# Running logsumexp over rows: first rows looked at by ScalarE, and another order of tile sizes

## The chip, the cores and the metric

The kernel runs on one NeuronCore of a Trainium2 chip. The metric is the device time of one execution in microseconds (us), lower is better. Beside the timed runs there is a profiled execution, whose trace holds each engine's instructions and the packets of the DMA engines. The engines are TensorE (PE in the profile), VectorE (DVE), ScalarE (ACT), GpSimd (POOL) and SyncE (SP), which here issues all transfers.

## What is computed

The input x has 4 batches of 4096 rows with 4128 columns, float32. Each output row is the logsumexp of all input rows up to it, column by column:

```python
out[:, 0, :] = x[:, 0, :].copy()
for t in range(1, S):
    mx = np.maximum(out[:, t - 1, :], x[:, t, :])
    out[:, t, :] = mx + np.log(np.exp(out[:, t - 1, :] - mx) + np.exp(x[:, t, :] - mx))
```

That is log(cumsum(exp(x))) over the rows. The input is 270.5 MB and so is the output; each is moved once.

## The kernel before, in words

**Tiles.** A batch's 4096 rows are cut into tiles of 2 or 3 blocks; a block is 128 rows. A tile of r blocks takes 128*r rows, and each of the 128 partitions holds r neighbouring rows of it (`dram`, L76). The class `Step` is such a tile: `b` is its batch, `row` its first row, `r` its number of blocks, and `first` and `last` say whether it begins or ends a batch. The lists `usual` (batches 0 to 2) and `final` (batch 3) give the sizes, in blocks, in order (L144 to L150). There are 49 tiles: 19 of two blocks and 30 of three. In this text tile 0 is the first, and load t and store t are its transfers.

**Buffers.** Four tiles are in the chip's SBUF at a time (`SLOTS`). Every fourth tile comes from the pool `x2`, which has room for two blocks, the others from `x3` with three buffers of three blocks.

**Work on one tile.** The columns are cut into three chunks of 1376 (`Chunk`). For each:
- `exp` (L97): ScalarE replaces the tile by its exponentials. In the first tile of a batch, the first row is also looked at: GpSimd compares its exponentials with 2^-63 (L99, into `ample`) and multiplies the answers into `least` (L103), so that `least` tells at the end whether any was too small.
- `sums` (L109, L111): VectorE adds the rows that lie in one partition, into `z` of this chunk. For three blocks L109 adds the first two in place, then L111 adds the last.
- `head` (L119): TensorE multiplies `z` by a triangular matrix, which gives each partition the sum of all rows before its own. In the first tile of a batch the matrix is `below`, in later ones `carried`, which also takes up the running sum that the tile before left in the last partition of `z`. The result is in PSUM (`pt`, two buffers). For a chunk these are two float32 products of 512 columns and one of 352, which the profile counts as six matmuls.
- `add` (L128, L136; in the last tile of a batch L131 in place of L136): VectorE adds that base to the tile's rows and puts the last row of each partition into `z`. L131 also adds up the result into `probe`.
- `log` (L141, L142): ScalarE takes the logarithm of all rows but the partition's last from the tile, and of the last from `z`, in place.

**What sets the order.** The order is written out by hand (`manual_schedule`), one list for each engine. ScalarE's list goes: for tile t, exp of chunk 2, log of chunk 0, exp of chunk 0 of the next tile, log of chunk 1, exp of chunk 1 of the next tile, log of chunk 2. VectorE's and TensorE's lists go beside it (L177 to L182). Every engine works its list in order. A look on GpSimd is issued with its `exp`, and VectorE's additions that overwrite the looked-at row come after it.

All transfers are issued by SP, in the order of `moves`: the loads of the first four tiles; store 0; store 1; and from there a load, three tiles ahead, behind each store. A store waits for the tile's three logarithms; a load waits for the store of the tile that had its buffer. An issue that waits holds back all that stand behind it in SP's list.

**At the end** (L213 to L234) the minimum over `least` (L215) and a comparison of `probe` with 2^62 (L218) go into the table `fits`, whose minimum over all partitions decides a flag. If the flag is set, a slow general version (`_general`) computes everything again; with the input at hand it is not.

Of the kernel before, what the change touches and what calls it, by code (L numbers as in the profile page):

```python
# [7 lines left out]
FP32 = mybir.dt.float32  # L8
I32 = mybir.dt.int32
ACT = mybir.ActivationFunctionType  # L10
ALU = mybir.AluOpType
AX = mybir.AxisListType
P = 128
MM = 512
NC = 3
SLOTS = 4
SMALL = 2.0 ** -63
LARGE = 2.0 ** 62
# [3 lines left out]
def kernel(  # L22
# [5 lines left out]
    nc = tc.nc  # L28
    B, S, D = x.shape
    assert S % P == 0 and D % (NC * 32) == 0  # L30
    CH = D // NC
# [3 lines left out]
    consts = ctx.enter_context(tc.tile_pool(name="consts", bufs=1))  # L35
# [10 lines left out]
        out=below, in_=below, pattern=[[1, P]], compare_op=ALU.is_ge,  # L46
# [5 lines left out]
        out=carried, in_=below, pattern=[[0, P]], compare_op=ALU.not_equal,  # L52
# [4 lines left out]

    probe = consts.tile([P, B * NC], FP32, name="probe")
    nc.gpsimd.memset(probe, 1.0)
    least = consts.tile([1, CH], FP32, name="least")  # L60
    nc.gpsimd.memset(least, 1.0)  # L61
    ample = consts.tile([1, CH], FP32, name="ample")

    z = [zpool.tile([P, CH], FP32, name=f"z{c}") for c in range(NC)]
    for t in z:
# [23 lines left out]
    class Chunk:  # L89
# [4 lines left out]
        def exp(self):  # L94
            t = self.t
            e = t.xt[:, :, self.cols]
            nc.scalar.activation(e, e, ACT.Exp)  # L97
            if t.first:
                nc.gpsimd.tensor_scalar(  # L99
                    out=ample, in0=t.xt[0:1, 0, self.cols], scalar1=SMALL, scalar2=None,  # L100
                    op0=ALU.is_ge,
                )
                nc.gpsimd.tensor_tensor(out=least, in0=least, in1=ample, op=ALU.mult)  # L103

        def sums(self):
            r = self.t.r
# [34 lines left out]
            nc.scalar.activation(e, e, ACT.Ln)  # L141
            nc.scalar.activation(t.xt[:, r - 1, self.cols], self.z, ACT.Ln)  # L142

    usual = [2, 3, 3, 3, 2, 3, 2, 3, 2, 3, 3, 3]  # L144
    final = [2, 3, 2, 3, 2, 2, 3, 2, 2, 3, 3, 3, 2]
    steps = []
    for b in range(B):
        parts = final if b == B - 1 else usual
        row = 0
        for i, r in enumerate(parts):  # L150
            if row == S:
                break
            pool = x3 if len(steps) % SLOTS else x2
            steps.append(Step(b, row, r, pool, row + P * r == S))
            row += P * r
        assert row == S
# [41 lines left out]
    while any(at[e] < len(l) for e, l in lists.items()):  # L198
        before = len(done), sum(at.values())
        for e, l in lists.items():  # L200
            while at[e] < len(l):
                op = l[at[e]]
# [7 lines left out]
        assert before != (len(done), sum(at.values()))  # L210


    fits = consts.tile([P, B * NC + 1], FP32, name="fits")  # L213
    nc.vector.memset(fits[:, B * NC:], 1.0)
    nc.vector.tensor_reduce(  # L215
        out=fits[0:1, B * NC:], in_=least, op=ALU.min, axis=AX.X,
    )
    nc.vector.tensor_scalar(  # L218
        out=fits[:, :B * NC], in0=probe, scalar1=LARGE, scalar2=None, op0=ALU.is_le,
    )  # L220
    low = consts.tile([P, 1], FP32, name="low")
    nc.vector.tensor_reduce(out=low, in_=fits, op=ALU.min, axis=AX.X)  # L222
# [4 lines left out]
        out=flag, in0=good, scalar1=float(P), scalar2=None, op0=ALU.is_lt,  # L227
# [68 lines left out]
```

## Time and profile before

| | |
|---|---|
| time, median of 3 runs | 1275.89 us (1275.76 to 1276.1) |
| profiled execution | 1275.27 us |
| span of its instructions | 1273.6 us |
| VectorE busy | 993.9 us, 548 instructions |
| ScalarE busy | 938.3 us, 442 instructions |
| TensorE matmuls busy | 609.9 us |
| GpSimd busy | 108.7 us, of it L99 57.9 us (12 times) and L103 45.0 us (12 times) |
| moved by DMA | 541.29 MB, 425 GB/s over the span |
| granted TensorE clock, mean | 0.69 |

The span goes from the first to the last instruction of the profiled execution; the rest of that execution's time, 1.67 us, lies around it. Busy time is the sum over an engine's instructions, and engines work at the same time, so the busy times do not add up to the span. In the profile a line such as `xt<-pt,xt` names the tile written and the tiles read. The time of a transfer is counted on 16 DMA engines; a DMA share of 1.00 in a stretch means that all 16 had packets throughout. (In stretches of one or two us a share can pass 1, because a packet counts where it starts.)

The most frequent instructions, by shape: Exp of three blocks takes 3633 ns and of two blocks 2486 ns (L97); the logarithm 2494 ns on two rows per partition and 1343 ns on one (L141), and 1335 ns from `z` (L142); VectorE's additions of 1376 columns take 1583 ns (L128 with one row per partition) and with two rows 3018 ns.

### The profile page before, as it was taken

How to read it: one execution, taken by the hardware profiler on the slowest of the kernel's cores; microseconds unless marked ns; L12 is line 12 of the kernel's file. 1: busy time of each engine (PE TensorE's matmuls, PEld its weight loads, DVE VectorE, ACT ScalarE, POOL GpSimd, SP SyncE). 2: the span in 40 equal slices, each digit the busy share in tenths (PEclk: the TensorE clock that was granted, in tenths of full speed). 3: DMA queues.
4: the chain of work that ended last, by engine and by line, in shares of the span. 5: the costliest groups of instructions: out<-in, count | busy, mean ns of one | idle time of the engine just before them, and what ended most of it. 6: DMA issues, size and time to landing. Idle time of an engine off the chain costs nothing.

```text
span 1273.6 us, 3466 instructions
## 1 busy us (share of the span) xinstructions
PE 609.9 (48%) x884; PEld 237.6 (19%) x884; DVE 993.9 (78%) x548; ACT 938.3 (74%) x442; POOL 108.7 (9%) x37
## 2 busy tenths in 40 slices
PE   2555445445445444644544545443553455362552
PEld 1222112212112111211211212111221122121220
DVE  4998668779779676867977959666997696784894
ACT  3798778678668677768956868766886686795894
POOL 6200000001600000000340000000043000000000
PEclk9667667666666767766666766776666767686676
DMA  9979999999999999999999999999999999999998
GB/s 407 420 318 422 425 437 429 434 431 426 439 433 427 431 433 429 438 430 437 431 430 433 431 433 432 433 433 429 434 440 425 439 429 435 425 411 415 429 442 345
DMA packets 14132, 541.29 MB, mean 425 GB/s; under 512 B 1568, under 2 KB 1568, under 8 KB 1568
## 3 DMA queue, kind: packets, MB, share of 16 engines
q1 hardware_dynamic: 14112, 541.07, 98.9%
q8 instruction: 7, 0.11, 0.0%
q14 instruction: 13, 0.11, 0.0%
HBM read 270.53 MB, written 270.53 MB: 425 GB/s over the span
## 4 chain that ended last, share of the span: by engine, by line
DMA 66%; DVE 19%; ACT 12%; issue 1%; PE 1%; SPq 0%; ACTq 0%; DVEq 0%
DMA xt<-in_x_dram 54%; DMA out_dram<-xt 13%; DVE xt L128 7%; ACT xt L97 5%; DVE z L111 5%; ACT xt L141 4%; DVE z L136 3%; DVE xt L109 3%; ACT xt L142 2%; PE pt L119 1%; DVE z L131 0%; SPq L87 0%; ACTq L141 0%; ACTq L97 0%; SPq L84 0%
## 5 line engine op out<-in xcount | busy, mean ns | idle before, releaser
L119 PE MATMUL pt<-z,carried 128*128 128x512 f32 (+1 forms) x810 | 557.3, 849 | 581.4 <-DVE z L111 581.4
L97 ACT ACTIVATE xt<-xt 128x4128 f32<-128x4128 f32 (+1 forms) x147 | 468.5, 3189 | 237.7 <-DMA xt<-in_x_dram 237.7
L119 PEld LDWEIGHTS pt<-z,carried 128*128 128x128 f32 x810 | 216.8, 285 | 922.0 <-issue 917.6
L128 DVE TENSOR_TENSOR xt<-pt,xt 128x2752 f32<-128x2752 f32 (+1 forms) x147 | 361.8, 2461 | 0.7 <-PE pt L119 0.7
L141 ACT ACTIVATE xt<-xt 128x2752 f32<-128x2752 f32 (+1 forms) x147 | 301.0, 2048 | 81.3 <-DVE z L136 76.3
L111 DVE TENSOR_TENSOR z<-xt 127x1376 f32<-127x1376 f32 x147 | 259.8, 1768 | 58.2 <-ACT xt L97 54.6
L109 DVE TENSOR_TENSOR xt<-xt 128x1376 f32<-128x1376 f32 x90 | 145.7, 1619 | 199.5 <-ACT xt L97 199.5
L136 DVE TENSOR_TENSOR z<-xt 128x1376 f32<-128x1376 f32 x135 | 224.2, 1660 | 4.6
L142 ACT ACTIVATE xt<-z 128x1376 f32<-128x1376 f32 x147 | 196.3, 1335 | 0.0
L99 POOL TENSOR_SCALAR ample<-xt 1x1376 f32<-1x1376 f32 x12 | 57.9, 4827 | 855.8 <-ACT xt L97 855.1
L119 PE MATMUL pt<-z,below 128*128 128x512 f32 (+1 forms) x72 | 52.4, 895 | 60.6 <-DVE z L111 60.6
L103 POOL TENSOR_TENSOR least<-least,ample 1x1376 f32<-1x1376 f32 x12 | 45.0, 3750 | 1.0
L119 PEld LDWEIGHTS pt<-z,below 128*128 128x128 f32 x72 | 20.7, 306 | 91.8 <-issue 70.8
L131 DVE CUSTOM_DVE_ANT_0 z<-xt 128x1376 f32<-128x1376 f32 x12 | 19.1, 1592 | 0.4
L66 POOL MEMSET z<- 128x1376 f32 x3 | 3.7, 1235 | 0.0
L224 PE MATMUL good<-ones,low 128*1 128x1 f32 x2 | 0.2, 164 | 5.6 <-DVE low L222 5.6
L34 ACT ACT_TABLE_LOAD x1 | 1.3, 1283 | 0.8 <-PEq L280 0.8
L215 DVE TENSOR_REDUCE fits<-least 1x1 f32<-1x1376 f32 x1 | 1.6, 1575 | 0.1
L224 PEld LDWEIGHTS good<-ones,low 128*1 128x1 f32 x2 | 0.1, 80 | 6.2 <-DVE low L222 6.2
L61 POOL MEMSET least<- 1x1376 f32 x1 | 1.2, 1235 | 0.0
L131 DVE DVE_READ_ACCUMULATOR2_ANT probe<- 128x1 f32 x12 | 1.0, 83 | 0.0
L226 DVE TENSOR_SCALAR flag<-good 1x1 int32<-1x1 f32 x1 | 0.1, 145 | 0.3 <-PE good L224 0.3
(12 smaller groups left out, 1.8 us busy)
## 6 DMA issues: line engine op xcount, KB each, us to landing
xt<-in_x_dram SPq DMA_DIRECT2D x30, 6192.0 KB, 38.6
out_dram<-xt SPq DMA_DIRECT2D x30, 6192.0 KB, 24.5
xt<-in_x_dram SPq DMA_DIRECT2D x19, 4128.0 KB, 33.9
out_dram<-xt SPq DMA_DIRECT2D x19, 4128.0 KB, 21.5
```

The costliest lines, as they stand in the source:

```text
L66: nc.gpsimd.memset(t, 0.0)
L97: nc.scalar.activation(e, e, ACT.Exp)
L99: nc.gpsimd.tensor_scalar(out=ample, in0=t.xt[0:1, 0, self.cols], scalar1=SMALL, scalar2=None, op0=ALU.is_ge,)
L103: nc.gpsimd.tensor_tensor(out=least, in0=least, in1=ample, op=ALU.mult)
L109: nc.vector.tensor_tensor(out=e[1], in0=e[0], in1=e[1], op=ALU.add)
L111: nc.vector.tensor_tensor(out=self.z[0:n], in0=e[r - 2][0:n], in1=e[r - 1][0:n], op=ALU.add,)
L119: nc.tensor.matmul(pt[:, a:b], lhsT=w, rhs=self.z[:, a:b], start=True, stop=True,)
L128: nc.vector.tensor_tensor(out=e, in0=base, in1=e, op=ALU.add)
L131: nc.vector.tensor_tensor_reduce(out=self.z, in0=ends[0], in1=ends[1], scale=1.0, scalar=0.0, op0=ALU.add, op1=ALU.add, accum_out=probe[:, ...
L136: nc.vector.tensor_tensor(out=self.z, in0=ends[0], in1=ends[1], op=ALU.add)
L141: nc.scalar.activation(e, e, ACT.Ln)
L142: nc.scalar.activation(t.xt[:, r - 1, self.cols], self.z, ACT.Ln)
```

## The change

Three things are edited. The first rows are looked at by ScalarE: after the exponential of a chunk in the first tile of a batch, it computes Relu(2^-63 - e) for the first row and sums it over the columns into one element of `short`, one element for each batch and chunk. GpSimd's two instructions for each look are gone, and `least` and `ample` with them. The sizes of the tiles come in another order: `begin` holds for batch 0 and `usual` for the others. At the end, `short` is compared with 0 instead of taking the minimum of `least`.

```diff
-    least = consts.tile([1, CH], FP32, name="least")
-    nc.gpsimd.memset(least, 1.0)
-    ample = consts.tile([1, CH], FP32, name="ample")
+
+    short = consts.tile([1, B * NC], FP32, name="short")
+    spare = consts.tile([1, CH], FP32, name="spare")
+    tiny = consts.tile([1, 1], FP32, name="tiny")
+    nc.gpsimd.memset(short, 0.0)
+    nc.gpsimd.memset(tiny, SMALL)
...
             nc.scalar.activation(e, e, ACT.Exp)
             if t.first:
-                nc.gpsimd.tensor_scalar(
-                    out=ample, in0=t.xt[0:1, 0, self.cols], scalar1=SMALL, scalar2=None,
-                    op0=ALU.is_ge,
+                k = t.b * NC + self.c
+                nc.scalar.activation(
+                    spare, t.xt[0:1, 0, self.cols], ACT.Relu, bias=tiny, scale=-1.0,
+                    accum_out=short[:, k:k + 1],
                 )
-                nc.gpsimd.tensor_tensor(out=least, in0=least, in1=ample, op=ALU.mult)
...
-    usual = [2, 3, 3, 3, 2, 3, 2, 3, 2, 3, 3, 3]
-    final = [2, 3, 2, 3, 2, 2, 3, 2, 2, 3, 3, 3, 2]
+    begin = [2, 2, 2, 3, 2, 3, 2, 3, 2, 3, 3, 3, 2]
+    usual = [3, 2, 3, 2, 3, 3, 3, 2, 3, 3, 3, 2]
     steps = []
     for b in range(B):
-        parts = final if b == B - 1 else usual
         row = 0
-        for i, r in enumerate(parts):
+        for r in usual if b else begin:
             if row == S:
                 break
             pool = x3 if len(steps) % SLOTS else x2
...
-    fits = consts.tile([P, B * NC + 1], FP32, name="fits")
+    fits = consts.tile([P, 2 * B * NC], FP32, name="fits")
     nc.vector.memset(fits[:, B * NC:], 1.0)
-    nc.vector.tensor_reduce(
-        out=fits[0:1, B * NC:], in_=least, op=ALU.min, axis=AX.X,
-    )
     nc.vector.tensor_scalar(
         out=fits[:, :B * NC], in0=probe, scalar1=LARGE, scalar2=None, op0=ALU.is_le,
+    )
+    nc.vector.tensor_scalar(
+        out=fits[0:1, B * NC:], in0=short, scalar1=0.0, scalar2=None, op0=ALU.is_le,
     )
```

There are again 49 tiles, 19 of two blocks and 30 of three, and the last four are of 3, 3, 3 and 2 blocks in both. Three of the four batches now begin with a tile of three blocks, and every batch ends with one of two.

More of the change, by code (lines that the diff above doesn't have):

```diff
@@ L210 @@
         assert before != (len(done), sum(at.values()))
-    fits = consts.tile([P, B * NC + 1], FP32, name="fits")
+    fits = consts.tile([P, 2 * B * NC], FP32, name="fits")
     nc.vector.memset(fits[:, B * NC:], 1.0)
-    nc.vector.tensor_reduce(
-        out=fits[0:1, B * NC:], in_=least, op=ALU.min, axis=AX.X,
+    nc.vector.tensor_scalar(
+        out=fits[:, :B * NC], in0=probe, scalar1=LARGE, scalar2=None, op0=ALU.is_le,
     )
     nc.vector.tensor_scalar(
-        out=fits[:, :B * NC], in0=probe, scalar1=LARGE, scalar2=None, op0=ALU.is_le,
+        out=fits[0:1, B * NC:], in0=short, scalar1=0.0, scalar2=None, op0=ALU.is_le,
     )
```

## The prediction, made before the changed kernel ran

> **What bounds the kernel now.** I read the page first: busy shares, then the slices, then the chain that ended last.
>
> ```profile
> PE 609.9 (48%) x884; PEld 237.6 (19%) x884; DVE 993.9 (78%) x548; ACT 938.3 (74%) x442; POOL 108.7 (9%) x37
> ...
> DMA  9979999999999999999999999999999999999998
> GB/s 407 420 318 422 425 437 429 434 431 426 439 433 427 431 433 429 438 430 437 431 430 433 431 433 432 433 433 429 434 440 425 439 429 435 425 411 415 429 442 345
> ...
> DMA 66%; DVE 19%; ACT 12%; issue 1%; PE 1%; SPq 0%; ACTq 0%; DVEq 0%
> ```
>
> No engine is full, but the DMA row is at 9 everywhere except in the third slice and the last, and two thirds of the chain are transfers. 541 MB must move whatever the tiles are, so time can only come from stretches in which the DMA engines stand still. Next I asked for the DMA share in windows (us from A to B, length, busy time and count per engine, TensorE clock, DMA share, GB/s).
>
> ```profile
> 130.00:1040.00 910.00, 441.38 (x630) 172.13 (x630) 718.52 (x393) 678.82 (x316) 78.32 (x18) 0.67 1.00 432
> 1115.00:1135.00 20.00, 13.42 (x24) 5.44 (x24) 18.18 (x12) 20.00 (x12) 0.00 (x0) 0.83 0.95 409
> 1240.00:1250.00 10.00, 5.92 (x11) 2.31 (x10) 8.44 (x7) 9.99 (x6) 0.00 (x0) 0.80 0.79 342
> ...
> 66.00:67.00 1.00, 1.00 (x3) 0.42 (x2) 1.00 (x1) 1.00 (x2) 0.00 (x0) 0.74 0.38 165
> 67.00:68.00 1.00, 1.00 (x2) 0.45 (x2) 1.00 (x1) 1.00 (x1) 0.00 (x0) 0.50 0.01 0
> ...
> 73.00:74.00 1.00, 0.61 (x1) 0.50 (x2) 1.00 (x2) 1.00 (x2) 0.00 (x0) 0.65 0.00 0
> ```
>
> For 910 us in the middle the share is 1.00 at 432 GB/s. The losses are: 0.62 + 0.99 + six empty windows = 7.6 us between 66 and 74; 0.05 x 20 = 1.0 us around 1123; 0.21 x 10 = 2.1 us around 1244. What releases the first gap stands in the timeline of the issuing queue and of ScalarE (start, length, engine, line, what):
>
> ```profile
> 49.76 24.55 SPq L87 DMA_DIRECT2D out_dram<-xt  x2
> 74.41 0.38 SPq L84 DMA_DIRECT2D xt<-in_x_dram  x1
> ...
> 48.40 1.33 ACT L142 ACTIVATE xt<-z 128x1376 f32<-128x1376 f32 x1
> ...
> 72.61 1.33 ACT L142 ACTIVATE xt<-z 128x1376 f32<-128x1376 f32 x1
> ```
>
> Store 0 goes out at 49.76, when ScalarE's last logarithm of tile 0 ends. Store 1 goes out just before load 4 (74.41), when the last logarithm of tile 1 ends at 73.94. In between the four first loads and store 0 are all the engines have. At 432 GB/s a tile of two blocks (4.23 MB) takes 9.8 us, one of three (6.34 MB) 14.7: 9.8 + 3 x 14.7 + 9.8 = 63.7 us of work, which ended at 66.6, so the engines began at 2.9.
>
> Why tile 0 is so late is seen on GpSimd and VectorE:
>
> ```profile
> 23.37 4.90 POOL L99 TENSOR_SCALAR ample<-xt 1x1376 f32<-1x1376 f32 x1
> 28.36 3.70 POOL L103 TENSOR_TENSOR least<-least,ample 1x1376 f32<-1x1376 f32 x1
> ...
> 29.04 4.47 DVE L111 TENSOR_TENSOR z<-xt 127x1376 f32<-127x1376 f32 x1
> ...
> 56.27 1.59 DVE L111 TENSOR_TENSOR z<-xt 127x1376 f32<-127x1376 f32 x1
> ```
>
> With GpSimd's looks running, an addition of two SBUF operands takes 4.47 us; the same addition takes 1.59 once they are over. Tile 0 and the start of tile 1 have four such additions (L111 three times, L109 once) and two slowed by 0.45 and 1.25 (L136): 4 x 2.9 + 1.7 = 13.3 us of VectorE time, at the very place that holds store 0.
>
> **The change, part by part.** *The looks.* 24 GpSimd instructions (57.9 + 45.0 us) go. Twelve ScalarE instructions on 1x1376 come. No row shows a Relu with a sum. Bounds: 0 from below (an instruction added to an in-order queue can be covered, but gains nothing), and from above L99's 4.83 us for the same 1x1376. I take 1.34, the row nearest in engine and length (L142, 1335 ns on 128x1376). So 16 us more on ScalarE in all; three of the twelve lie in the start, 4.0 us.
>
> The Trainium skill ("ScalarE: Activation LUTs", What ACT_TABLE_LOAD costs) has a rule that would speak against this: every switch to a different table set costs about 2.66 us. The same page (Table sets: the hidden batching unit) says that Relu is filler in every set. By the first sentence alone, three looks with a switch there and back would put 6 x 2.66 = 16 us (estimate) into the start, for a time near 1281; by the second, nothing. The trace of before has one load of 1.28 us (L34), with 441 Exps and Lns after it, and shows no Relu.
>
> *The start, worked forward.* Rows: Exp of two blocks 2.5, of three 3.63; the pair of Ln on a two-block tile 2.6 (29.21 to 31.71, plus its end); additions 1.59; a head of six matmuls 4.97 as the first one had; a look 1.34. Load 0 lands at 13.2 as now.
> - Tile 0, ScalarE: Exp to 15.7, look to 17.1, Exp to 19.6, look to 20.9, Exp to 23.4, look to 24.8. VectorE and TensorE beside it: sum 15.8 to 17.4, head to 22.4, two additions to 25.6. Ln of chunk 0 to 28.3, Exp of tile 1 to 30.8, Ln of chunk 1 to 33.4 (its additions end at 30.6), Exp to 35.9, Ln of chunk 2 (ready at 35.7) to 38.5. **Store 0 at 38.6** instead of 49.76.
> - Tile 1 (two blocks now): ScalarE has three times Exp and Ln without a gap, 3 x 5.1 = 15.3; TensorE 3 x 4.97 = 14.9 and VectorE 3 x 4.8 = 14.3 lie beside it. **Store 1 at 54.0** instead of 74.0.
> - Tile 2, with two Exps of the three-block tile 3: 2.5 + 7.8 + 7.3 = 17.6. **Store 2 at 71.6.**
> - Tile 3 goes at VectorE's pace for three blocks, 7.69 us per chunk (58.47 to 66.16 on ScalarE): **store 3 by 94.7.**
>
> The DMA engines meanwhile: loads 2.9 + 3 x 9.8 + 14.7 = 47.0; store 0 to 56.8. Store 1 is needed by then; issued at 54.0, it flows 0.8 later, at 54.8: 2.0 us to spare. It lasts to 66.6. Load 4 waits on SP for store 0's landing (about 58), behind store 1 in order: to 76.4. Store 2 (71.6) is in time by 4: to 86.2; load 5 to 100.9; store 3 (94.7) in time by 5. What SP holds behind each waiting store is the next load, and the DMA engines have work during each of these waits. The 7.6 us go.
>
> *The order of sizes.* 49 tiles before and after, 19 of two blocks and 30 of three: the same transfers, so no term for bytes. From the fifth tile on the sizes run through the same cycle of twelve (2,3,2,3,2,3,3,3,2,3,3,3) as now from the fifth tile, where the share is 1.00. The pairs 2,2 of the last batch, where the 1.0 us around 1123 was lost with less in flight, are gone: gain 1.0, bounds 0 and 1.0. Later batches begin with three blocks; SP's store before them comes after two looks, 2.7 us later. In the same place of the cycle now, a store issued at 797.39 is followed by a load for which the Exp at 833.66 waits: 36.3 us, less 24.5 for the two transfers and 2.6 of latency (load 0: 13.24 - 0.82 - 9.8), leave 9 us of older transfers in the queue, so the 2.7 are covered; uncovered they would cost 3 x 2.7 = 8 us.
>
> *The rest.* L215 (1.57 us) becomes a comparison of 12 elements (L218: 0.15); it runs at 1255 to 1258, under the last stores, which end near 1271. Gain 0; without that cover 1.4. The memset of 1.24 us goes, under the first load. The tail keeps its 3,3,3,2: the Exp that follows the last three-block load waits for it now (1.45 us before 1208.38) and will, so the 2.1 us around 1244 stay.
>
> **Sum.** The profiled execution took 1275.27 us (span 1273.6 and 1.67 around it); the median of three is 0.6 above it, 1275.89. Span: 1273.6 - 7.6 - 1.0 = 1265.0; median: 1275.9 - 8.6 = **1267.3**.
>
> **Rivals.** *Store 1 is late and part of the gap stays.* For it: only 2.0 us to spare, and the look is unmeasured. Against: the heads were taken at their slowest. Each microsecond beyond costs one: looks of 2.7 instead of 1.34 make it 4 us late and leave 2: 1269.3; looks of 3.2 leave 3.7: 1271.
>
> *Relu brings table loads.* Two of 1.28 (L34) at each look: 7.7 us in the start, 5.7 beyond the reserve, and about 1 us at each later batch: 1267.3 + 5.7 + 3 = 1276, no change. For: nothing in the rows; against: the built program of the changed kernel holds one load only.
>
> *The gap is covered anyway.* If compute set the end, an earlier start of the stores would be given back: 1275.9. For: the chain's last 60 us are compute. Against: VectorE is at 78%, ScalarE waits 237.7 us for loads, up to the Exp at 1208.
>
> *The smaller start runs dry: slower.* Nine blocks are loaded ahead instead of eleven, 9.8 us less work in the queue. If store 1 stays late, the gap grows: it equals the old 8.6 when store 1 is issued at 54.0 + 2.0 + 8.6 = 64.6, and with store 1 at 74 as now the time is 1267.3 + 18 = 1285. It takes looks that hold ScalarE about 4.9 us each, L99's price; at 6 us, 1279. For: the looks stand ahead of Exp and Ln on an in-order engine. Against: 1.34 us rows.
>
> **How the numbers follow.** Forecast 0.70; late store 1 0.18; table loads 0.03; covered anyway 0.04; runs dry 0.05. 0.2% (2.6 us) is about what a measurement of this kernel tells from no change. Faster: the first two and a little, 0.88; same: 0.07; slower: 0.05. Range: below, the tail's 2.1 us gone too, 1265.2; above, the late store to 1271.0.
>
> **What would show it.** Right: no empty 1 us window between 40 and 110; store 0 near 39, store 1 near 54; additions of 1.6 us at the start; looks near 1.34 and one table load; the middle still at 432 GB/s; the loss around 1244 unchanged. Wrong: a gap before store 1 (looks or heads dearer), gaps at 320, 640 or 960 (looks uncovered), or the last load's Exp no longer waiting.

## The result, and the profile after

The changed kernel takes 1262.68 us (median of 4 runs, 1262.57 to 1262.9), the kernel before 1275.94 us. The ratio is 0.9896, with a 95% interval from 0.9879 to 0.9913. The forecast was 1267.3 us with a range down to 1265.2: the direction was right, but the gain was 13.3 us instead of 8.6, and the time lies below the range.

The page of the changed kernel, busy rows and DMA slices, as they were shown of before:

```profile
PE 604.6 (48%) x884; PEld 235.2 (19%) x884; DVE 955.3 (76%) x548; ACT 955.4 (76%) x466; POOL 4.6 (0%) x14
...
DMA  9999999999999999999999999999999999999998
GB/s 402 419 444 425 437 425 434 431 428 435 433 430 439 423 436 439 428 436 434 428 436 427 438 426 436 439 432 433 431 433 426 435 433 436 428 436 435 429 425 348
...
DMA 70%; ACT 14%; DVE 14%; issue 0%; PE 0%; SPq 0%; ACTq 0%; DVEq 0%
```

The 7 in the third DMA slice is gone (318 GB/s became 444). VectorE lost 39 us of busy time, ScalarE gained 17, and the span still follows the transfers. Two slices of before also rose, which the prediction had passed over: the 36th and 37th, 411 and 415 GB/s with a DMA row of 9, now 436 and 435.

The start in the timelines of SP and ScalarE (start, length, engine, line, what):

```profile
38.10 15.04 SPq L90 DMA_DIRECT2D out_dram<-xt  x2
58.25 0.34 SPq L87 DMA_DIRECT2D xt<-in_x_dram  x1
70.34 0.33 SPq L90 DMA_DIRECT2D out_dram<-xt  x1
...
15.72 1.44 ACT L103 ACTIVATE spare<-xt,tiny 1x1376 f32<-1x1376 f32 x1
17.07 0.18 ACT L103 ACTIVATION_READ_ACCUMULATOR spare<-xt,tiny 1x1 f32 x1
17.16 2.48 ACT L100 ACTIVATE xt<-xt 128x2752 f32<-128x2752 f32 x1
```

Store 0 goes out at 38.1 and store 1 at 52.8 (38.10 + 15.04, less its own 0.34), against 49.8 and 74.0 before. A look is an activation of 1.44 us and a readout of the sum of 0.18 us, and the next Exp begins 1.44 after the look began.

Where the time came from is seen best in windows over the two places where before lost time. The last two columns are the DMA share and GB/s; first before, then after:

```profile
57.00:130.00 73.00, 42.11 (x60) 15.84 (x60) 66.51 (x36) 62.27 (x29) 0.00 (x0) 0.71 0.90 377
1040.00:1165.00 125.00, 56.92 (x91) 22.29 (x90) 83.29 (x51) 88.88 (x49) 0.00 (x0) 0.70 0.99 420
```

```profile
57.00:130.00 73.00, 37.79 (x60) 14.85 (x60) 61.30 (x35) 59.23 (x30) 0.00 (x0) 0.74 1.01 433
1040.00:1165.00 125.00, 60.60 (x88) 23.85 (x89) 100.39 (x56) 93.70 (x42) 0.00 (x0) 0.68 1.00 433
```

By the share, before lost 0.10 x 73 = 7.3 and 0.01 x 125 = 1.3 us. By the bytes, against the 432 GB/s of the undisturbed middle, it lost (1 - 377/432) x 73 = 9.3 and (1 - 420/432) x 125 = 3.5 us, together 12.8. The span fell by 1273.6 - 1260.9 = 12.7 us. So the bytes account for the gain, and 4.2 us of it were lost while the DMA engines counted as busy: packets took longer there.

The agreement is closer than the method: a window counts a packet where it starts, and one round of 16 packets at an edge is worth up to 1.8 us, the time of one packet. The page's line on the queue has no such edges. It gives packets, MB and the time that the packets took, as a share of 16 engines over the whole span; here of before, of the changed kernel, and of the changed kernel run once more (after_2, span 1261.4 us):

```profile
q1 hardware_dynamic: 14112, 541.07, 98.9%
...
q1 hardware_dynamic: 14112, 541.07, 99.5%
...
q1 hardware_dynamic: 14112, 541.07, 99.6%
```

The same packets took 0.989 x 1273.6 = 1259.6 us in before, 0.995 x 1260.9 = 1254.6 in the changed kernel and 0.996 x 1261.4 = 1256.4 in its repeat. The rest of each span, 14.0, 6.3 and 5.0 us, the engines were idle. So 8 to 9 us of the gain are idle time, and 3 to 5 us are packets that no longer take longer than usual.

The slow packets show in two short windows of before, just ahead of and at the end of store 1, the transfer that ended the first empty stretch. Each line gives packets, MB and the time that the packets took, as a share of 16 engines over the 2 us of the window:

```profile
q1 hardware_dynamic: 16, 0.79, 92.0%
...
q1 hardware_dynamic: 16, 0.79, 128.2%
```

The 16 packets that start in 84.9 to 86.9 took 0.920 x 2 = 1.84 us each; the 16 that start in 86.5 to 88.5 took 2.56. All are of the same size.

At the second place only part of the engines had run empty: 4 or 5 of the 16 still had a packet under way at 1123 to 1124 us. In the window from 1137.1 to 1138.1 us 13 packets start, in the next 1 us the other three:

```profile
q1 hardware_dynamic: 13, 0.64, 216.0%
...
q1 hardware_dynamic: 3, 0.15, 34.4%
```

The 13 took 2.16 x 16 / 13 = 2.66 us each, the three 0.344 x 16 / 3 = 1.83. So here it is not the moment that is slow for all: the engines whose packets start within the same half microsecond are slow together, and the other three run as always.

### The profile page after: what moved, and what is told of

Same layout as the page of the kernel before. It is cut to its first block, busy times and chain, and to the rows that moved or that the text cites. A ratio compares the mean times of both kernels' runs of the same rounds, so it can differ in the third digit from the quotient of the medians.

```text
span 1260.9 us, 3429 instructions
## 1 busy us (share of the span) xinstructions
PE 604.6 (48%) x884; PEld 235.2 (19%) x884; DVE 955.3 (76%) x548; ACT 955.4 (76%) x466; POOL 4.6 (0%) x14
## 4 chain that ended last, share of the span: by engine, by line
DMA 70%; ACT 14%; DVE 14%; issue 0%; PE 0%; SPq 0%; ACTq 0%; DVEq 0%
DMA xt<-in_x_dram 54%; DMA out_dram<-xt 15%; ACT xt L100 6%; DVE xt L131 6%; ACT xt L144 5%; DVE z L114 3%; DVE z L139 3%; ACT xt L145 3%; DVE xt L112 1%; PE pt L122 0%; SPq L90 0%; DVE z L134 0%; ACTq L233 0%; ACTq L144 0%; ACTq L100 0%
## 5 line engine op out<-in xcount | busy, mean ns | idle before, releaser
L112 DVE TENSOR_TENSOR xt<-xt 128x1376 f32<-128x1376 f32 x90 | 142.8, 1586 | 223.5 <-ACT xt L100 223.5
L114 DVE TENSOR_TENSOR z<-xt 127x1376 f32<-127x1376 f32 x147 | 233.9, 1591 | 58.0 <-ACT xt L100 53.8
L139 DVE TENSOR_TENSOR z<-xt 128x1376 f32<-128x1376 f32 x135 | 214.9, 1592 | 4.6
L103 ACT ACTIVATE spare<-xt,tiny 1x1376 f32<-1x1376 f32 x12 | 17.3, 1441 | 0.5
```

Source lines behind the costliest of these rows:

```text
L103: nc.scalar.activation(spare, t.xt[0:1, 0, self.cols], ACT.Relu, bias=tiny, scale=-1.0, accum_out=short[:, k:k + 1],)
L112: nc.vector.tensor_tensor(out=e[1], in0=e[0], in1=e[1], op=ALU.add)
L114: nc.vector.tensor_tensor(out=self.z[0:n], in0=e[r - 2][0:n], in1=e[r - 1][0:n], op=ALU.add,)
L139: nc.vector.tensor_tensor(out=self.z, in0=ends[0], in1=ends[1], op=ALU.add)
```

## The experiments

Two theories stood against each other. G: a stretch in which the DMA engines have nothing to do costs its own length, and about 2 us more behind the restart. P: the slow packets belong to the pattern of tile sizes, and the empty stretches cost only their length. The changed kernel is the point of comparison, with 1262.7 us; beside the last runs it took 1263.2.

**looks_only**: the looks on ScalarE, the sizes as before.

```diff
-    begin = [2, 2, 2, 3, 2, 3, 2, 3, 2, 3, 3, 3, 2]
-    usual = [3, 2, 3, 2, 3, 3, 3, 2, 3, 3, 3, 2]
+    usual = [2, 3, 3, 3, 2, 3, 2, 3, 2, 3, 3, 3]
+    final = [2, 3, 2, 3, 2, 2, 3, 2, 2, 3, 3, 3, 2]
...
-        for r in usual if b else begin:
+        for i, r in enumerate(parts):
```

> Only the looks go to ScalarE, the order of sizes is the old one. Theory G (a stretch without DMA work costs its own length and about 2 us more, because packets behind the restart run slower): with tile 0 done near 38 and tile 1 (three blocks) near 62, store 1 is in time for the 66.6 at which the DMA engines run out, so the whole first loss (7.6 empty, 1.9 in slow packets) goes and the second, of about 3.5 in all around 1123 to 1160, stays: 1266.4 us. Theory P (the slow packets belong to the pattern of sizes, here a three-block store before a two-block load, and not to the empty stretch): only the 7.6 us go, 1268.3 us, and packets of store 1 and load 4 stay slow.

Measured: 1266.65 us, 0.9924 of before (0.9907 to 0.994). The time is the one that G gave, but the packets are not. Windows of this run, and its line on the queue:

```profile
57.00:130.00 73.00, 37.12 (x54) 14.11 (x54) 59.95 (x33) 59.77 (x28) 0.00 (x0) 0.69 1.01 427
1040.00:1165.00 125.00, 55.24 (x93) 22.24 (x93) 84.84 (x52) 88.85 (x48) 0.00 (x0) 0.69 1.00 422
75.00:100.00 25.00, 14.96 (x22) 5.47 (x20) 24.76 (x15) 22.19 (x11) 0.00 (x0) 0.70 1.00 401
1115.00:1116.00 1.00, 1.00 (x2) 0.34 (x1) 0.99 (x1) 1.00 (x2) 0.00 (x0) 0.50 0.38 165
...
q1 hardware_dynamic: 14112, 541.07, 99.6%
```

At the first place no engine ran empty any more: store 1 went out at 65.2, just before the 66.6 at which the engines ran out in before. Yet the packets there were as slow as in before: 75 to 100 us had 401 GB/s at a share of 1.00, so (1 - 401/432) x 25 = 1.8 us were lost. (The window from 57 to 130 shows only 0.8 us, which is an effect of its edges.) At the second place part of the engines still ran empty, as the share of 0.38 shows, and 2.9 us were lost.

Over the whole span of 1264.3 us the packets took 0.996 x 1264.3 = 1259.2 us, within rounding the 1259.6 of before. So what this run gained was idle time. That slow packets stay at the first place is what P expected, while P's time, 1268.3, was missed by some 1.7 us; G's time came out, but G expected those packets to go, so its agreement is partly luck. This run alone does not decide between the two. It shows that slow packets also come where no engine has run empty, which G as written does not say.

**sizes_only**: the new sizes, the looks on GpSimd as before.

```diff
-    usual = [2, 3, 3, 3, 2, 3, 2, 3, 2, 3, 3, 3]
-    final = [2, 3, 2, 3, 2, 2, 3, 2, 2, 3, 3, 3, 2]
+    begin = [2, 2, 2, 3, 2, 3, 2, 3, 2, 3, 3, 3, 2]
+    usual = [3, 2, 3, 2, 3, 3, 3, 2, 3, 3, 3, 2]
```

> Only the order of sizes is new, the looks stay on GpSimd. Tile 0 is done near 47.5 and tile 1 near 62.5, and the DMA engines run out at 56.8. Theory G: an empty stretch of about 6.5 us and 2 us of slow packets behind it, none around 1123: 1271 us. Theory P: the slow packets of before do not come back with the new order, 1269 us.

Measured: 1287.85 us, 1.0086 of before (1.0069 to 1.0102). Half of the change, alone, makes the kernel slower by 11.5 us. Both expectations missed it, because they saw only the start. The windows show four places:

```profile
45.00:95.00 50.00, 29.99 (x53) 12.05 (x52) 47.23 (x30) 45.86 (x25) 0.00 (x0) 0.79 0.85 347
340.00:400.00 60.00, 31.32 (x48) 12.50 (x49) 56.21 (x30) 44.46 (x22) 9.85 (x3) 0.72 0.94 392
660.00:720.00 60.00, 36.64 (x51) 14.38 (x52) 56.44 (x30) 45.79 (x23) 8.79 (x2) 0.66 0.95 395
980.00:1040.00 60.00, 33.80 (x54) 13.30 (x54) 56.19 (x29) 47.20 (x24) 7.18 (x2) 0.74 0.95 398
```

By the bytes they lose 9.8 + 5.6 + 5.1 + 4.7 = 25.2 us, and 1262.7 + 25.2 = 1287.9. By the share they lose 7.5 + 3.6 + 3.0 + 3.0 = 17.1: 2 us at each place are slow packets, also at those that have no counterpart in before. The changed kernel has the same sizes and 433 GB/s between 130 and 1040 us, so the sizes alone do not make packets slow: P falls with this. The three later places are the starts of batches 1 to 3, where GpSimd's looks now meet tiles of three blocks. VectorE's timeline there:

```profile
342.44 3.01 DVE L128 TENSOR_TENSOR xt<-pt,xt 128x2752 f32<-128x2752 f32 x1
345.48 1.59 DVE L136 TENSOR_TENSOR z<-xt 128x1376 f32<-128x1376 f32 x1
346.99 4.49 DVE L109 TENSOR_TENSOR xt<-xt 128x1376 f32<-128x1376 f32 x1
```

With three blocks both L109 and L111 read two tiles from SBUF, and such additions take up to 4.5 us beside a look, while L128, with one operand from PSUM, keeps its 3.01. The Trainium skill ("SBUF — State Buffer", Who interferes with whom) says that a VectorE instruction with two SBUF inputs contends with a GpSimd instruction that reads SBUF, and that the port pair which they share is an exclusive lock; the 4.49 us of L109 and the unchanged 3.01 us of L128 agree. How much of each place's idle time these additions make was not worked out.

**gap_small** and **gap_large**: the changed kernel with an empty stretch made in the middle of the run, by 5 or 11 needless instructions on ScalarE.

```diff
             e = t.xt[:, 0:r - 1, self.cols]
+            if t is steps[17] and self.c == NC - 1:
+                for _ in range(5):
+                    nc.scalar.activation(spare, spare, ACT.Relu)
             nc.scalar.activation(e, e, ACT.Ln)
```

> The changed kernel with five needless Relus (1x1376) on ScalarE ahead of the last logarithm of tile 17, about 7 us. Store 17 had 3.9 us to spare, so about 2 us of empty DMA time come in the middle of the run, with no other change. Theory G: 2 us and about 2 us of slow packets behind it, 1266.5 us. Theory P: 2 us alone, 1264.7 us.

> As gap_small with eleven Relus, about 15 us: some 10 us of empty DMA time. Theory G: the surcharge does not grow with the length, 10 + 2: 1275 us. Theory P: 1273 us. If the surcharge grows in proportion with the empty time (9.5 for 7.6 in the first loss), 1275 as well, but then gap_small has a surcharge of only 0.5, 1265.2 us.

Measured: 1267.2 and 1275.6 us; repeated later beside gap_split, gap_large took 1275.16.

> gap_large again, beside gap_split on the same chip: 1275.6 us, with about 2 us in slow packets behind the restart.

The same window of the changed kernel, of gap_small and of gap_large, in this order:

```profile
450.00:520.00 70.00, 33.54 (x48) 13.25 (x48) 53.39 (x30) 53.54 (x25) 0.00 (x0) 0.69 1.00 432
```

```profile
450.00:520.00 70.00, 31.32 (x48) 12.20 (x48) 53.06 (x29) 56.74 (x29) 0.00 (x0) 0.74 0.98 412
```

```profile
450.00:520.00 70.00, 32.32 (x49) 12.63 (x48) 53.52 (x29) 63.65 (x34) 0.00 (x0) 0.68 0.86 359
```

By share the two lose 1.4 and 9.8 us, by bytes 3.2 and 11.8: the surcharge is about 2 us at either length. Nothing but the empty stretch was added, at a place where the sizes are those of the changed kernel. So an empty stretch brings the surcharge with it, and it does not grow with the length of the stretch. The times grew a little more than the windows show: by 4.5 and 12.9 us against 1262.7, and gap_large_2 by 12.0 against after_2 on the same chip, where its window loses 11.3. Where the remaining 0.7 to 1.3 us lie was not found.

An empty stretch is not the only place for slow packets, though. These are the last 16 packets of load 3, ahead of store 0, in before (the 2 us from 54 to 56), in the changed kernel (from 44.4) and in sizes_only (from 43.5):

```profile
q1 hardware_dynamic: 16, 0.79, 142.4%
...
q1 hardware_dynamic: 16, 0.79, 139.3%
...
q1 hardware_dynamic: 16, 0.79, 91.5%
```

In the first two, store 0 was already queued (issued at 49.8 and 38.1), and the packets took 2.85 and 2.79 us, although the engines had not been empty since the first load began. In sizes_only store 0 was issued only at 48.2, when load 3 had ended, and the packets took 1.83 us. What these cases and the restarts have in common is that all engines go over from a load to a store, or back, at nearly one moment: the 16 packets of the changed kernel start within 0.5 us. That this is the cause is argued from the traces; no experiment here shows it.

**gap_split**: as gap_large, with store 17 in two transfers, of 8 and 120 partitions.

```diff
+            if self is steps[17]:
+                for part in (slice(0, 8), slice(8, P)):
+                    nc.sync.dma_start(out=self.dram(out)[part], in_=self.xt[part])
+                return
             nc.sync.dma_start(out=self.dram(out), in_=self.xt)
```

> As gap_large (the same empty stretch of some 9 to 10 us before store 17), but store 17 goes out as two transfers, the first with 8 of the 128 partitions. If the slow packets come from all 16 DMA engines changing from store 17 to load 20 at one moment, an uneven first transfer lets some change earlier than others, and most of the 2 us behind the gap should go: some 2 us below gap_large, and few slow packets at the end of store 17. If they come from the empty stretch as such, or from the order store, load, the time is that of gap_large.

Measured: 1297.07 us, 22 more than gap_large. The experiment does not decide what it was made for: the uneven transfers brought a much larger loss of their own (the section on the hardware has it). Whether the slow packets come from all engines changing from a store to a load at one moment is left open; the 13 and 3 packets and the end of load 3 speak for it.

**looks_four** and **looks_none**: four looks for each chunk of the first batch, and no look at all (the guard against too small first rows left out).

```diff
-                nc.scalar.activation(
-                    spare, t.xt[0:1, 0, self.cols], ACT.Relu, bias=tiny, scale=-1.0,
-                    accum_out=short[:, k:k + 1],
-                )
+                for _ in range(1 if t.b else 4):
+                    nc.scalar.activation(
+                        spare, t.xt[0:1, 0, self.cols], ACT.Relu, bias=tiny, scale=-1.0,
+                        accum_out=short[:, k:k + 1],
+                    )
```

> The changed kernel with each look of the first batch made four times: nine more of about 1.5 us on ScalarE, so store 1 goes out near 66 instead of 52.8, and the DMA engines run out at about 57. Theory G (empty time plus about 2 us behind the restart): some 9 to 10 us empty, 1274 us. One for one, as the prediction priced it: 1272 us.

> The changed kernel without the look at the first rows: that part of the computation (the guard against too small first rows) is left out. If the three looks at the start and the later ones lie under transfers, as the trace of the changed kernel says (store 1 meets 4.3 us of queued transfers), the time is the same, 1262.7 us. If they still cost, it is shorter by up to 4 us.

Measured: 1274.64 and 1263.43 us. The twelve looks cost nothing as they are, since store 1 has some 3.5 us to spare. With 13.7 us more of them ahead of store 1 (it goes out at 66.5) the time grows by 12.0 us, and lies 11.2 above looks_none on the same chip. One for one, as the prediction had it, it would be 13.7 - 3.5 = 10.2; the surcharge is the difference, 1 to 1.8 us here.

**start_2323**: the first batch without any two-block neighbours.

```diff
-    begin = [2, 2, 2, 3, 2, 3, 2, 3, 2, 3, 3, 3, 2]
+    begin = [2, 3, 2, 3, 2, 3, 2, 3, 2, 3, 2, 3, 2]
```

> The changed kernel with the first batch in tiles of 2,3,2,3,2,3,2,3,2,3,2,3,2: no two-block neighbours anywhere, and ten blocks loaded ahead instead of nine, but tile 1 has three blocks. Store 1 near 62.5, the DMA engines run out near 61.8. Theory G: an empty stretch of 1 to 2 us and 2 us of slow packets, 1266 us. If only the late neighbours had mattered: 1262.7 us.

Measured: 1266.66 us, as G has it. SP issues store 1 at 63.5, after the queue has run empty. With a second tile of three blocks the start is too slow even with the looks on ScalarE, so the three tiles of two blocks have a part in the gain.

**tail_split**, **tail_one** and **after_2**: an attempt at the loss that both kernels keep, before store 47. The last two tiles, or only tile 47, are stored in two transfers, chunk 0 ahead of the others.

```diff
+        if t >= n - 2:
+            moves += [("part", t, 0), ("rest", t)]
+            continue
         moves.append(("store", t))
```

> The changed kernel with the last two tiles stored in two transfers each: chunk 0 when its logarithm is done, chunks 1 and 2 later. The 2.6 us without transfers before store 47 should be filled: 1260.1 us if pieces of 5.5 and 11 KB move as fast as the pieces of 33 and 49.5 KB of the other transfers; if they are slower by a quarter, about 1265 us.

> As tail_split, but only tile 47 is stored in two transfers; the last store is whole, so that the end is not spread over small pieces. If the small pieces at the very end ate the gain of tail_split: 1261 us. If filling the gap before store 47 brings nothing because the pieces of 5.5 and 11 KB cost what was gained: 1262.7 us or more.

> The changed kernel itself, beside tail_one on the same chip: 1262.7 us.

Measured: 1263.56, 1263.12 and 1263.17 us. The stretch before store 47 is filled, but nothing is gained. Windows of the changed kernel and then of tail_one:

```profile
1220.00:1240.00 20.00, 13.72 (x22) 5.09 (x21) 18.34 (x14) 16.07 (x10) 0.00 (x0) 0.74 0.85 367
1240.00:1261.00 21.00, 0.19 (x2) 0.09 (x2) 2.97 (x8) 4.56 (x4) 0.00 (x0) 0.60 0.82 353
```

```profile
1220.00:1240.00 20.00, 13.25 (x24) 5.09 (x22) 18.34 (x12) 16.75 (x9) 0.00 (x0) 0.80 0.95 405
1240.00:1262.00 22.00, 0.34 (x3) 0.09 (x2) 4.28 (x10) 5.18 (x4) 0.00 (x0) 0.62 0.72 306
```

From 367 to 405 GB/s ahead of 1240, but from 353 to 306 behind it. The reason stands in the timeline of tail_one:

```profile
1245.08 1.33 ACT L153 ACTIVATE xt<-z 128x1376 f32<-128x1376 f32 x1
...
1246.44 0.34 SPq L90 DMA_DIRECT2D out_dram<-xt  x1
```

The last store goes out when ScalarE's last logarithm ends, at 1246.4 here and at 1245.1 in the changed kernel, and in both the span ends 15.7 to 15.8 us later. Storing a part of tile 47 earlier does not move that logarithm, so the idle time only moves behind it. No run beat the changed kernel.

## Why the prediction was right in direction and wrong in size

- *What bounds the kernel*: right. Transfers set the time, and all that the change gained lies in the two places that were named; between 130 and 1040 us the rate is 433 GB/s after and 432 before.
- *The losses*: this step failed. "0.62 + 0.99 + six empty windows = 7.6 us between 66 and 74; 0.05 x 20 = 1.0 us around 1123" counts empty time by the DMA share, and a slow packet counts as busy there: its term was put at nothing. By bytes the two places lose 9.3 and 3.5 us, 12.8 instead of 8.6. The page had it: GB/s 411 and 415 in two slices with a 9, and the window from 75 to 100 had 391 GB/s at a share of 0.98. The empty stretch made by hand (gap_large) and the three new ones (sizes_only) show the surcharge of about 2 us each. Why the packets are slow stays open. With the surcharge the prediction's own sum is 1275.9 - 12.8 = 1263.1.
- *The looks*: a look is 1.44 us instead of 1.34, plus 0.18 for the sum, and the next Exp begins 1.44 after it. The Trainium skill ("ScalarE: Activation LUTs", What ACT_TABLE_LOAD costs) gives 280 ns + 0.833 ns an element for an activation whose bias is a pointer, by which a look would be 1.43 us (an estimate from the skill's figures); the trace, with 1.44, agrees. One table load stands in the trace, 1.28 us, so that rival did not come. looks_none shows that the looks are covered.
- *The start, worked forward*: right. Forecast and measured: store 0 at 38.6 and 38.1, store 1 at 54.0 and 52.8, store 2 at 71.6 and 70.3. The additions are back at 1.59 us, as expected.
- *The order of sizes*: the sign was right with the looks on ScalarE, but the reason was incomplete. "Later batches begin with three blocks" was treated as free. It is, because the looks left GpSimd: with them there, each of the three starts costs 5 us (sizes_only). The two parts of the change do not add up: the looks alone gain 9.7 us, the sizes alone lose 11.5, and together they gain 13.3. The cycle of sizes was also misread: its first pass has eight tiles in the changed kernel, not twelve. Nothing was lost there.
- *The smaller start runs dry*: did not happen in the changed kernel, but it is what sizes_only does in its first 100 us, with store 1 only at 62.9. There the rival's price, 1:1 from the reserve on, is again too small: 62.9 - 56.0 = 6.9 us, against 9.8 by the bytes.
- *The tail*: right. The Exp behind the last three-block load still waits for it (2.02 us at 1195.4), and the loss before store 47 stays.

## What to carry to other kernels

Where transfers bound a kernel, count lost time by the bytes that did not move, not by the time that the engines were idle: busy engines may be slow, and here a third of the loss lay there. An empty stretch brought about 2 us of slow packets with it, so filling a short gap can bring twice its length; but where it was only just filled (looks_only), the slow packets stayed. And a new order of sizes is judged together with what else runs at the same places: here it was worth 4 us beside one form of the looks and cost 11.5 beside the other.

## What the runs showed of the hardware

Behind an empty stretch the packets at the next changes between store and load took 1.4 times their usual time on average (in before 2.56 instead of 1.84 us); about 2 us in all, whether 1.4 or 9.8 us had been empty. The engines were closer in step ahead of this than behind it: in before the 16 packets at 87.7 us start within 0.2 us, those at 99.0 within 0.9. The same slow packets came at the first change from load to store, with nothing empty before it (2.79 us in the changed kernel). After an empty stretch that ended with a store alone (store 0 in sizes_only, nothing queued behind it) the packets ran at their normal pace: 128 of them, with 16 small ones, took 89.7% of 11 us, 1.23 us each.

In gap_split, a store of 8 partitions and one of 120 in place of one of 128 cut the rate by some two fifths for about 40 us. The packets that start between 474 and 506 us, of gap_split and then of gap_large_2:

```profile
q1 hardware_dynamic: 201, 7.79, 96.1%
```

```profile
q1 hardware_dynamic: 346, 13.44, 102.9%
```

The engines are as busy, but move 7.79 MB instead of 13.44: 2.45 us a packet against 1.52. Why was not tried.
